# A second copy of k's low part, so that both score products of an attention block take all 128 rows of the array

## The chip, the cores and the metric

The kernel runs on one core of a Trainium2 chip. The time is that of one execution on the device in microseconds (us). The kernel before took 3684.35 us as the median of three runs (3678.03 to 3684.88).

The core has five engines, each with its own queue of instructions that it takes in order: TensorE (PE in the profile) multiplies a moving tile with weights that were loaded into its 128x128 array beforehand (PEld), VectorE (DVE), ScalarE (ACT) and GpSimd (POOL) work elementwise, and SyncE (SP) issues most of the transfers (DMAs). Products land in PSUM, which VectorE and ScalarE read.

## The reference

Two layers of a transformer trunk work on 1024 latent tokens and 256 context tokens of width 1024. In each layer a token mixer (a recurrent part A, a windowed attention B, a neighbourhood attention C) is followed by a mixture of 32 experts. The change touches the scores of the attentions B and C. For the windowed attention the reference computes

```
s_loc = jnp.einsum('bnqhgd,bnkhd->bnhgqk', qb, kb).astype(F32) * ATTN_SCALE
s_ctx = jnp.einsum('bnqhgd,bmhd->bnhgqm', qb, kc).astype(F32) * ATTN_SCALE
p = jax.nn.softmax(jnp.concatenate([s_loc, s_ctx, sink_col], -1), -1).astype(v.dtype)
o = (jnp.einsum('bnhgqk,bnkhd->bnqhgd', p[..., :nk], vb)
     + jnp.einsum('bnhgqm,bmhd->bnqhgd', p[..., nk:nk + L], vc))
```

with heads of 64 numbers. Attention C has the same form with a bias table and no sink.

## The kernel before

q and k are float32 numbers that are stored in two float16 parts: a high part (z = 0) and a low part (z = 1), which is what the high part leaves over. A score q·k is then a sum of products of parts, accumulated in PSUM.

The function `attention` works through six groups in each layer (three of B, three of C), two heads (e = 0, 1) a group. Layer 0 has 10 blocks of 128 queries in a group, layer 1 has 8. For a group these tiles are loaded:

- `qs` (128 partitions): the high part of q in partitions 0 to 63, the low part in 64 to 127.
- `k1` (128 partitions): the high part of k, twice, once in either half (L1100).
- `kl` (64 partitions): the low part of k, once (L1102).
- `vt`: the values.

The groups of B share one load of k, each group of C has its own, so there are four loads of `kl` in a layer.

For each block and head the scores are made in up to three pieces of 256 or 128 keys. A piece is a pair of products into the same PSUM region: L1149 multiplies all 128 rows of `qs` with `k1` (high·high plus low·high), and L1150 multiplies the 64 rows of q's high part with `kl` (high·low). Every product loads its weights, a slice of `qs`, anew. VectorE then adds the mask or bias and finds the maximum (L1162), ScalarE takes the exponential (L1168), GpSimd multiplies with the inverse of the sum (L1179), TensorE transposes the probabilities in pieces of 128 (L1182, L1187), ScalarE and VectorE copy the transposed pieces out of PSUM (L1183, L1188), TensorE multiplies with the values (L1192), whose products use 128 rows and 64 columns of the array, and ScalarE and VectorE write the result in two parts (L1199, L1200). Three blocks can be under way (tiles with three buffers); the scores have two PSUM buffers.

During the groups of B the output of part A (`rwkv_out`, L964 to L1015) runs between the blocks on the same engines. After the last group `out_proj` (L1277) multiplies with the output weights, and the experts follow.

Within a queue the order is fixed when the program is built: a scheduler with a model of the engines lays all instructions of a stage into the queues. A change in a transfer or an operation can therefore move other instructions too.

Of the kernel before, what the change touches and what calls it, by code (L numbers as in the profile page):

```python
# [10 lines left out]
F16 = mybir.dt.float16  # L11
# [10 lines left out]
T = S + L  # L22
P = 128
# [265 lines left out]
class Trunk:  # L289
# [774 lines left out]
    def attention(self, l, ap, qp, sets, with_ctx, groups, depth):  # L1064
        nc = self.nc
        v, g, a, te = nc.vector, nc.gpsimd, nc.scalar, nc.tensor
# [9 lines left out]
        elif groups[0] < 3:  # L1076
            sk, sks, bm = self.attB
            k1, kl, vt = self.attkv
# [5 lines left out]
        for grp in groups:  # L1084
            B = grp < 3
# [5 lines left out]
            qs = qp.tile([P, 2, T], F16, tag="qs", name="qs", bufs=2)  # L1091
# [4 lines left out]
            if not B or i == 0:  # L1096
                kd = self.qkv[c + "k", i].rearrange("(e p) z t -> z p e t", e=2)
                k1 = qp.tile([P, 2, T], F16, tag="k1", name="k1", bufs=1 if B else 2)
                for z in range(2):
                    nc.sync.dma_start(k1[64 * z:64 * z + 64], kd[0])  # L1100
                kl = qp.tile([64, 2, T], F16, tag="kl", name="kl", bufs=1 if B else 2)
                nc.sync.dma_start(kl, kd[1])  # L1102
                vt = qp.tile([P, NT, P], F32, tag="vt", name="vt", bufs=1 if B else 2)
                vd = self.qkv[c + "v", i]
                nb = NT if B else 2
                nc.sync.dma_start(vt[:, 0:nb], vd[0:nb * P].rearrange("(b p) v -> p b v", p=P))

                vg = vd[L:T].rearrange("(r c j) v -> c r j v", c=8, j=8)
                for b in range(nb, NT):
                    nc.sync.dma_start(vt[:, b], vg[b - 2])  # L1110
                self.attkv = k1, kl, vt
# [15 lines left out]
            for blk in range(0 if with_ctx else 2, NT):  # L1127
# [11 lines left out]
                Q = slice(blk * P, blk * P + P)  # L1139
# [6 lines left out]
                for e in range(2):  # L1146
                    pss = ps_s.tile([P, 1024], F32, tag="s", name="pss")
                    for o, k0, n in pieces:
                        te.matmul(pss[:, o:o + n], qs[:, e, Q], k1[:, e, k0:k0 + n], start=True, stop=False)  # L1149
                        te.matmul(pss[:, o:o + n], qs[0:64, e, Q], kl[:, e, k0:k0 + n], start=False, stop=True)  # L1150
                    if not lat:
                        bb = self.zrow.unsqueeze(1).to_broadcast([P, 2, P])
                        o_ap, i_ap = (z.rearrange("p (z k) -> p z k", z=2) for z in (s2[:, e, :nk], pss[:, 0:nk]))
                    else:
                        bb = bias[e][0 if 2 < blk < NT - 1 else 1]
                        o_ap, i_ap = s2[:, e, :nk], pss[:, 0:nk]
                        if blk == 2:
                            bb = bass.AP(tensor=bb.tensor, offset=bb.offset, ap=[bb.ap[0], [384, 2], [1, 256]])
                            o_ap, i_ap = (z.rearrange("p (z k) -> p z k", z=2) for z in (o_ap, i_ap))
                        else:  # L1160
                            bb = bb[:, :nk]
                    v.tensor_tensor_reduce(out=o_ap, in0=i_ap, in1=bb, op0=OP.add, op1=OP.max, scale=1.0,  # L1162
                                           scalar=sks[:, heads[e]:heads[e] + 1] if B else NEG, accum_out=mx[:, e:e + 1])
# [26 lines left out]
                for x, kb in enumerate(kbs):  # L1190
                    for e in range(2):
                        te.matmul(po[64 * e:64 * e + 64, 0:P], vt[:, kb, 64 * e:64 * e + 64], pt[:, e, x * P:x * P + P],  # L1192
                                  start=x == 0, stop=x == len(kbs) - 1)
# [841 lines left out]
```

## Time and profile before

| | |
|---|---|
| median of three runs | 3684.35 us |
| the profiled execution | 3684.05 us, its span 3682.0 us |
| attention, layer 0 | 732.1 to 1035.5 us of the span |
| attention, layer 1 | 2551.0 to 2827.4 us |
| products of L1149 and of L1150 | 552 each |
| granted TensorE clock, mean of the span | 0.91 |

Times in rows are counted from the start of the span. In the rows of an engine's timeline the start of an instruction is measured, while the length given for a matmul is a model that includes the way through the array: successive matmuls overlap. What a matmul takes of TensorE is read from the distance of its start to the next one's. "128*128" and "64*128" are rows and columns of the array that the weights fill. [...]

### The profile page before, as it was taken

To read this page: it belongs to the slowest core of one execution; us is meant where nothing else is said; L and a number is where in the kernel's file an instruction comes from. 1 tells how busy PE (TensorE), PEld (TensorE's weight loads), DVE (VectorE), ACT (ScalarE), POOL (GpSimd) and SP (SyncE) were. 2 spreads that over 40 slices of the span, in tenths; PEclk is the share of its full clock that TensorE was granted. 3 is DMA by queue.
4 is the path that set the end of the run, shared out by engine and by line. 5 is a ranking of instruction groups with operands and counts; after the bars stand their busy time and mean duration, and the time that the engine had idled before them with its cause. 6 is when DMAs were issued, how large, how long until landed. Compare 5 with 4: busy or idle time off the path is not lost. (4 is left out here: it accounts for less than half of the span.)

```text
span 3682.0 us, 67190 instructions
## 1 busy us (share of the span) xinstructions
PE 3146.3 (85%) x26916; PEld 1837.6 (50%) x26916; DVE 1787.3 (49%) x4387; ACT 1090.0 (30%) x2416; POOL 915.9 (25%) x912
## 2 busy tenths in 40 slices
PE   7998889999997889999738988898999879986773
PEld 4656557656654344444326655675655444432331
DVE  4357777377668311111186677773755841110115
ACT  4333334346533100000045433442554310000001
POOL 2023433143324100000073244331432410000003
PEclk9989889989998899999968987997999879997987
DMA  9864333552264889989762533335331778899885
GB/s 361 298 185 113 88 87 95 147 152 67 79 206 166 275 334 360 368 347 358 293 223 74 158 94 98 94 89 163 96 106 57 254 238 344 330 386 360 308 317 196
DMA packets 456087, 770.06 MB, mean 209 GB/s; under 512 B 194398, under 2 KB 328830, under 8 KB 439134
## 3 DMA queue, kind: packets, MB, share of 16 engines
q1 hardware_dynamic: 442206, 718.16, 56.2%
q0 software_dynamic: 12848, 44.97, 3.8%
q8 instruction: 214, 3.51, 0.4%
q10 hardware_dynamic: 720, 2.62, 0.2%
q14 instruction: 99, 0.81, 0.1%
HBM read 650.68 MB, written 114.97 MB: 208 GB/s over the span
## 5 line engine op out<-in xcount | busy, mean ns | idle before, releaser
L1618 PE MATMUL pgate<-wg,hT 128*32 128x256 f32 (+2 forms) x1968 | 532.4, 487 | 85.9 <-issue 31.8
L1618 PEld LDWEIGHTS pgate<-wg,hT 128*32 128x32 f32 (+2 forms) x1968 | 196.3, 135 | 349.9 <-issue 287.7
L1618 PE MATMUL pgate<-wu,hT 128*32 128x256 f32 (+1 forms) x1648 | 361.6, 462 | 10.2 <-DMA wu<-w_up 10.2
L1639 PE MATMUL pd<-wd,gT 128*32 128x256 f32 (+2 forms) x1968 | 321.8, 472 | 51.7 <-DVE gT L1631 25.8
L514 PE MATMUL acc<-hL,wH 128*128 128x256 f16 (+2 forms) x1040 | 345.5, 333 | 16.3 <-POOL hL L471 16.2
L513 PE MATMUL acc<-hH,wH 128*128 128x256 f16 (+2 forms) x1040 | 343.3, 334 | 7.2 <-DVE hH L470 6.4
L515 PE MATMUL acc<-hH,wL 128*128 128x256 f16 (+2 forms) x1040 | 344.9, 333 | 0.0
L1623 ACT ACTIVATE sg<-pgate 64x256 f32<-64x256 f32 (+2 forms) x86 | 43.1, 501 | 980.3 <-PE pgate L1618 980.3
L1592 POOL DMA_INDIRECT xg<-hmoe,map x69 | 62.3, 903 | 1037.5 <-PE ptg L1628 566.3
L1179 POOL TENSOR_SCALAR s<-s,rd 128x640 f32<-128x640 f32 (+2 forms) x216 | 171.6, 795 | 288.4 <-DVE rd L1175 115.8
L1639 PEld LDWEIGHTS pd<-wd,gT 128*32 128x32 f32 (+2 forms) x1968 | 127.1, 130 | 208.7 <-issue 123.0
L1624 DVE TENSOR_TENSOR sg<-sg,pgate 64x256 f32<-64x256 f32 (+1 forms) x66 | 35.6, 540 | 344.4 <-ACT sg L1623 340.9
L1168 ACT ACTIVATE s<-s,nm 128x640 f32<-128x640 f32 (+2 forms) x216 | 164.4, 764 | 45.8 <-DVE nm L1165 39.8
L1277 PE MATMUL acco<-wo,o 128*128 128x512 f16 x756 | 176.5, 387 | 0.0
L1192 PE MATMUL po<-pt,vt 128*64 128x128 f32 x1920 | 168.6, 291 | 7.3 <-DVE pt L1183 6.5
L1618 PE MATMUL pup<-wu,hT 128*128 128x512 f32 x320 | 165.4, 605 | 9.6 <-DMA wu<-w_up 9.6
L1149 PE MATMUL pss<-k,qs 128*128 128x256 f16 (+1 forms) x552 | 153.2, 278 | 17.3 <-DMA k<-Bk 13.4
L1624 DVE TENSOR_TENSOR sg<-sg,pup 128x512 f32<-128x512 f32 x20 | 13.8, 688 | 292.1 <-PE pup L1618 292.1
L1618 PEld LDWEIGHTS pgate<-wu,hT 128*32 128x32 f32 (+1 forms) x1648 | 134.3, 123 | 42.1 <-issue 21.1
L1150 PE MATMUL pss<-kl,qs 64*128 64x256 f16 (+1 forms) x552 | 152.6, 277 | 0.0
L515 PEld LDWEIGHTS <-wL 128*128 128x128 f16 (+1 forms) x1040 | 104.9, 101 | 87.4 <-issue 26.7
L513 PEld LDWEIGHTS <-wH 128*128 128x128 f16 (+1 forms) x1040 | 105.4, 101 | 75.4 <-issue 19.7
(406 smaller groups left out, 6435.3 us busy)
## 6 DMA issues: line engine op xcount, KB each, us to landing
wu<-w_up SPq DMA_DIRECT2D x64, 2048.0 KB
wd<-w_down SPq DMA_DIRECT2D x64, 2048.0 KB
wg<-w_gate SPq DMA_DIRECT2D x64, 2048.0 KB
wmod<-w_mod SPq DMA_DIRECT2D x96, 512.0 KB
w<-w_in SPq DMA_DIRECT2D x41, 512.0 KB
ld<-ys SPq DMA_DIRECT2D x40, 384.0 KB
z<-inv SPq DMA_DIRECT2D x80, 128.0 KB
ys<-y SPq DMA_DIRECT2D x20, 512.0 KB
```

The source lines that it names most:

```text
L513: self.nc.tensor.matmul(ov, H[:, k, :], hh, start=k == 0, stop=False)
L514: self.nc.tensor.matmul(ov, H[:, k, :], hl, start=False, stop=False)
L515: self.nc.tensor.matmul(ov, Lo[:, k, :], hh, start=False, stop=k == KD - 1)
L1149: te.matmul(pss[:, o:o + n], qs[:, e, Q], k1[:, e, k0:k0 + n], start=True, stop=False)
L1150: te.matmul(pss[:, o:o + n], qs[0:64, e, Q], kl[:, e, k0:k0 + n], start=False, stop=True)
L1168: a.activation(s2[:, e, :nk], s2[:, e, :nk], AF.Exp, bias=nm[:, e:e + 1], scale=1.0 / SS, accum_out=den[:, e:e + 1])
L1179: g.tensor_scalar(s2[:, e, :nk], s2[:, e, :nk], rd[:, e:e + 1], SC_Q, OP.mult, OP.mult)
L1192: te.matmul(po[64 * e:64 * e + 64, 0:P], vt[:, kb, 64 * e:64 * e + 64], pt[:, e, x * P:x * P + P], start=x == 0, stop=x == len(kbs) - 1)
L1277: te.matmul(acc, o[:, zo, k] if k < KD - 1 else self.og_last[:, zo, tok], wo[:, zw, k, c], start=k == 0 and y == 0, stop=k == KD - 1 and y ...
L1592: nc.gpsimd.indirect_dma_start(out=xg[:m], out_offset=None, in_=self.h2[l], in_offset=bass.IndirectOffsetOnAxis(ap=idx, axis=0))
L1618: te.matmul(o[off + i * m:off + i * m + m, :n], hT[:, k], w[:, k, i * n:i * n + n], start=k == 0, stop=k == KD - 1)
L1639: te.matmul(o, gT[:, k, :m], wd[:, k, i * n:i * n + n], start=k == 0, stop=k == 3)
```

## The change

`kl` becomes a tile of 128 partitions, which two transfers fill with the same low part of k, and L1150 (L1151 now) multiplies all 128 rows of `qs` with it. It thereby also adds the product low·low. The weights of both products of a piece are now the same slice of `qs`. All line numbers from L1103 on are higher by one.

```
-                kl = qp.tile([64, 2, T], F16, tag="kl", name="kl", bufs=1 if B else 2)
-                nc.sync.dma_start(kl, kd[1])
+                kl = qp.tile([P, 2, T], F16, tag="kl", name="kl", bufs=1 if B else 2)
+                for z in range(2):
+                    nc.sync.dma_start(kl[64 * z:64 * z + 64], kd[1])
...
                         te.matmul(pss[:, o:o + n], qs[:, e, Q], k1[:, e, k0:k0 + n], start=True, stop=False)
-                        te.matmul(pss[:, o:o + n], qs[0:64, e, Q], kl[:, e, k0:k0 + n], start=False, stop=True)
+                        te.matmul(pss[:, o:o + n], qs[:, e, Q], kl[:, e, k0:k0 + n], start=False, stop=True)
```

On SyncE, ahead of the first group of layer 0, the queue before has these rows (`k_9029` is the tile `k1`, `Bk_0` the array with k, `Ck_0` an array with k of attention C that is still being written):

```order
L1095 DMA qs<-Bq_0_3628 64x1280 x4
L1100 DMA k_9029<-Bk_0_5158 64x2x1280 x2
L1102 DMA kl<-Bk_0_5158 64x2x1280
L1060 DMA Ck_0_8222<-qhl 256x1x512
L1106 DMA vt<-Bv_0_2957 128x10x128
L1095 DMA qs<-Bq_0_4138 64x1280 x4
```

and now these:

```order
L1095 DMA qs<-Bq_0_3628 64x1280 x4
L1100 DMA k_9029<-Bk_0_5158 64x2x1280 x2
L1103 DMA kl<-Bk_0_5158 64x2x1280
L1060 DMA Ck_0_8222<-qhl 256x1x512
L1103 DMA kl<-Bk_0_5158 64x2x1280
L1107 DMA vt<-Bv_0_2957 128x10x128
L1095 DMA qs<-Bq_0_4138 64x1280 x4
```

The second half of `kl` stands behind the store of `Ck_0`, and the values behind it.

On TensorE the pairs of the scores stay in their order, but the scheduler places the steps of `rwkv_out` and of the softmax differently between them. In the first group of layer 0 the second tile of `rwkv_out` (L992) stands here before:

```order
L1149 MATMUL pss<-k_9029,qs 128x128
L1150 LDWEIGHTS qs
L1150 MATMUL pss<-kl,qs 128x128
L1192 MATMUL po<-pt,vt 64x128 x3
L1182 MATMUL pp<-c_58,s_9115 128x128 x8
L992 MATMUL po<-c_58,yb 64x64 x16
L1149 LDWEIGHTS qs
L1149 MATMUL pss<-k_9029,qs 128x256
```

and here now:

```order
L1150 MATMUL pss<-k_9029,qs 128x128
L1151 LDWEIGHTS qs
L1151 MATMUL pss<-kl,qs 128x128
L1188 MATMUL pp_9272<-c_58,s_9228 128x128 x2
L1193 MATMUL po<-pt,vt 64x128 x8
L1183 MATMUL pp<-c_58,s_9289 128x128 x4
L992 MATMUL po<-c_58,yb 64x64 x16
L1193 MATMUL po<-pt,vt 64x128 x2
```

Ahead of that tile stand 20 pairs of scores before and 38 now, so it has moved back by three blocks.

## Rows read from the trace of the kernel before

**Rows 1.** The page: busy time of TensorE, its share of the span, instructions.

```profile
PE 3146.3 (85%) x26916; PEld 1837.6 (50%) x26916; DVE 1787.3 (49%) x4387; ACT 1090.0 (30%) x2416; POOL 915.9 (25%) x912
```

**Rows 2.** Busy time by stretch: first group, rest of B, C, for each layer.

```profile
core 0: us, PE busy (x) PEld busy (x) DVE busy (x) ACT busy (x) POOL busy (x), PEclk, DMA share, GB/s
732.10:789.40 57.30, 53.37 (x328) 29.67 (x325) 41.83 (x140) 25.73 (x72) 23.33 (x26) 0.79 0.73 190
789.40:889.20 99.80, 98.45 (x817) 60.30 (x815) 72.33 (x242) 55.35 (x162) 41.80 (x50) 1.00 0.21 64
889.20:1035.50 146.30, 141.79 (x1129) 89.49 (x1127) 91.72 (x270) 85.49 (x219) 53.53 (x72) 0.98 0.27 76
2551.00:2599.20 48.20, 48.20 (x274) 26.27 (x274) 28.49 (x91) 19.35 (x51) 14.41 (x16) 0.65 0.81 225
2599.20:2691.30 92.10, 91.66 (x769) 57.07 (x767) 64.55 (x215) 50.40 (x140) 38.75 (x44) 1.00 0.26 81
2691.30:2827.40 136.10, 130.65 (x1026) 82.80 (x1024) 79.71 (x216) 74.40 (x182) 44.26 (x60) 0.95 0.30 90
```

**Rows 3.** TensorE's longest waits, layer 0 then layer 1: total us, times, longest.

```profile
PE pss L1149 <- DVE mx L1162: 3.9, 4, 1.6
...
PE pss L1149 <- DMA k<-Bk: 13.4, 1, 13.4
PE po L1192 <- DVE pt L1183: 5.3, 8, 3.4
```

**Rows 4.** VectorE's waits in the attention of layer 0, same columns.

```profile
DVE pt L1183 <- PE pp L1182: 34.3, 32, 2.3
...
DVE s L1162 <- PE pss L1150: 14.3, 29, 1.4
```

**Rows 5.** TensorE's timeline, layer 0, group of C: start us, length us, instruction.

```profile
945.83 0.27 PE L1182 MATMUL pp<-c,s 128*128 128x128 f32 x1
945.94 0.27 PE L1149 MATMUL pss<-k,qs 128*128 128x256 f16 x1
946.14 0.28 PE L1150 MATMUL pss<-kl,qs 64*128 64x256 f16 x1
946.36 0.28 PE L1149 MATMUL pss<-k,qs 128*128 128x256 f16 x1
```

**Rows 6.** TensorE's timeline, layer 0, a piece of 128 keys.

```profile
858.35 0.23 PE L1149 MATMUL pss<-k,qs 128*128 128x128 f16 x1
858.51 0.23 PE L1150 MATMUL pss<-kl,qs 64*128 64x128 f16 x1
```

**Rows 7.** TensorE's timeline, layer 0, input projection, 256 columns.

```profile
699.54 0.27 PE L513 MATMUL acc<-hH,wH 128*128 128x256 f16 x1
699.65 0.27 PE L514 MATMUL acc<-hL,wH 128*128 128x256 f16 x1
```

**Rows 8.** TensorE's timeline, layer 0, input projection, 128 columns.

```profile
712.52 0.22 PE L524 MATMUL accn<-wH,hH 128*128 128x128 f16 x1
712.58 0.22 PE L525 MATMUL accn<-wH,hL 128*128 128x128 f16 x1
```

**Rows 9.** Lines L1149 and L1150: count, shortest/median/longest ns, first and last start.

```profile
L1149 PEld LDWEIGHTS <-qs x552: 95/96/152, 732.1 to 2815.7; 128*128 128x128 f16 x184
L1149 PE MATMUL pss<-k,qs x552: 219/282/421, 732.1 to 2815.7; 128*128 128x256 f16 x160, 128*128 128x128 f16 x24
...
L1150 PE MATMUL pss<-kl,qs x552: 226/280/417, 732.4 to 2815.9; 64*128 64x256 f16 x160, 64*128 64x128 f16 x24
```

**Rows 10.** Loads of kl: their issues on SyncE, and the size of one.

```profile
L1102 SPq DMA_DIRECT2D kl<-Bk x2: 573/574/574, 711.7 to 2546.4; - x2
...
kl<-Bk SPq DMA_DIRECT2D x1, 320.0 KB
```

**Rows 11.** TensorE's timeline, layer 1, first group, clock at half.

```profile
2557.78 0.40 PE L1149 MATMUL pss<-k,qs 128*128 128x256 f16 x1
2558.11 0.39 PE L1150 MATMUL pss<-kl,qs 64*128 64x256 f16 x1
```

## The prediction

> **What bounds the kernel now.** I began with the page's busy times: TensorE is busy for 85% of the span and none of the others for more than half of it [rows 1]. An average over stages does not say what an edit in attention is worth, so I read the busy times by stretch. In the six stretches of attention TensorE is busy in 564 of 580 us (their sum), VectorE in 65% on the whole, 73% in the first stretch [rows 2]. Next the waits. TensorE waits 13.4 us for k ahead of layer 1's first score, but within the attentions its longest entries are 3.9 and 5.3 us in total [rows 3]. VectorE stands for TensorE again and again: 34.3 us for transposes and 14.3 us for scores in layer 0 alone [rows 4]. TensorE therefore sets the pace here, and time taken from it can be gained.
>
> Busy matmuls overlap, so I then read distances between starts. After a transpose, which fills 128x128, the first score product starts 0.11 us later. From that product to its partner with 64 rows it is 0.20 us, and from there to the next one with 128 rows 0.22 us [rows 5]. In the input projection, where every product has 128 rows and its own weights too, products of the same 256 columns follow each other at 0.11 us [rows 7]. With 128 columns the same holds: 0.16 us from 128 to 64 rows [rows 6] against 0.06 us where the rows stay 128 [rows 8]. So each passage between 128 and 64 rows costs 0.16 - 0.055 = 0.215 - 0.11 = 0.105 us, whatever the number of columns, and in both directions. (0.215 and 0.055 are the means over a run of such starts; the rows round to hundredths.)
>
> **The change part by part.**
>
> *The passages.* There are 552 pairs [rows 9]. The old order of instructions has a passage inside each: 552. A second product is followed directly by the next pair's first one 392 times, and by a transpose with 128x128 65 times; those passages go too. Where a product with the values follows (128 rows, 64 columns; some 85 times) the array changes its shape as before, and I count nothing. That makes 1009 passages x 0.105 = 106 us of TensorE's time. With the clock at half the pair's distance is 0.33 us [rows 11] where 256 columns without a passage would take twice 0.11 = 0.22; the passage costs 0.11 us there as well, so one price will do.
>
> [...] The row first: the weight load of a score product takes 96 ns [rows 9], nearly the price of the passage, so the 0.105 us could be a load that is not hidden. [...] The trace disagrees: the projection's products share all rows and still follow at 0.11 us [rows 7]. [...]
>
> *How much of it reaches the end.* In proportion to the pairs (48 in a group of layer 0, 44 in layer 1) the six stretches of [rows 2] could lose 9.2, 18.4, 27.6, 8.4, 16.9 and 25.3 us. That leaves 48.1, 81.4, 118.7, 39.8, 75.2 and 110.8 us, in which VectorE's unchanged work fills 87, 89, 77, 72, 86 and 72%. [...] The products with the values wait for copies that stood behind 1.2 us of scores and now behind 0.55 us. Where VectorE comes to 85% or more I let 60% of the gain through, elsewhere 85%. Both shares are chosen; they lie between 100% and 40%. At 40% VectorE would be busy for (91.7 + 79.7) / (282.4 - 21.2) = 66% of the stretches of C, hardly more than the 61% of now, so less than that would need a cause that the rows don't show. The sum: 5.5 + 11.0 + 23.5 + 7.1 + 10.1 + 21.5 = 78.7 us. With 40% everywhere it would be 42, with all of it 106.
>
> *The loads.* Eight more transfers of 320 KB [rows 10]. At the rate of the two first groups, 190 and 225 GB/s [rows 2], one takes 1.7 and 1.5 us. In these groups the DMA engines are loaded to 73 and 81%, layer 1 waits for k as it is [rows 3], and the scores need both halves of `kl`; I put both on the path: 3.2 us. From below it is nothing, if other instructions fill the time. If the store of `Ck_0` ahead of the second half holds it up as well, I allow a second transfer's time, so 6.4 us is the upper bound. The six loads of C run ahead under groups whose transfers are busy for 21 to 30%; without that cover they would cost 6 x 1.6 = 10 us. The issue of a load, 0.6 us on SyncE [rows 10], lies ahead of the need except in the first groups, and is in the 3.2 us.
>
> *The order.* The steps of `rwkv_out` move back by some blocks in the groups of B. Their work is the same, and they still end within the B groups; I cost it at nothing. Its cover is TensorE's backlog; without this, VectorE's steps of one such tile would come in one piece ahead of a block's maximum. VectorE waits up to 2.3 us at a time now [rows 4], and with nine tiles 20 us is the worst, which is part of the rival on VectorE.
>
> *Sum.* 3684.05 - 78.7 + 3.2 = 3608.6 us on the profiled execution. That execution lies 0.3 us below the median of the runs, so I predict 3609 us. After the attention each layer goes on with the output weights and experts, whose loads wait for space that attention frees, so a saved microsecond passes on to the end.
>
> **The rivals.**
>
> *VectorE and the chain of softmax take over.* Only 40% of the gain gets through: 3684 - 42 + 3 = 3645 us. For it: VectorE at 86 to 89% in half of the stretches, and few buffers (two for scores, three blocks). Against it: 49 us of VectorE's idle time in layer 0 are waits for TensorE itself [rows 4], which shrink with it. Chance 0.19.
>
> *Everything gets through, and the clock gains.* In layer 1's first group the clock is granted at 0.65, after the wait of 13.4 us [rows 3], and it stays low while TensorE is shown as busy throughout [rows 2]; denser products may lift it earlier. If that group ran at full clock for half of its slow time it would be some 8 us: 3684 - 106 + 3 - 8 = 3573 us. Against it: the waits of [rows 3] grow when TensorE reaches them sooner. Chance 0.11.
>
> *The price is the weight load, not the change of rows.* Then the distances remain 0.2 us and only the transfers are added: 3684 + 3 = 3687 us. Against it: a score product behind a transpose, also with its own load, starts after 0.11 us [rows 5], and the projection keeps that pace [rows 7]. Chance 0.03.
>
> *The clock falls (slower).* TensorE with less to do waits more, and the clock of attention, 0.93 as the mean of [rows 2] weighted by length, falls. Its work at full clock would be about 580 - 106 = 474 us, and each share of it that moves to half clock costs as much again. If all six stretches had the 0.79 of the first, 2 x (0.93 - 0.79) = 0.28 more of it would be slow: 474 x 0.28 = 133 us, and the time 3684 - 103 + 133 = 3714 us. It decides from a mean clock of 0.93 - 103/474/2 = 0.82 on. For it: the lowest clock, 0.65, follows the longest wait. Against it: 1.00 in two stretches in spite of waits of up to 1.6 us [rows 2, 3]. Chance 0.04.
>
> **How the numbers follow.** The forecast has 0.63, with a range of its own of 3592 to 3629 us (from 90 to 55% of the 106 us in all stretches alike, with the 3.2 us for the loads). The range to hold 8 in 10 reaches to the rival on VectorE and to the one in which all gets through: 3572 to 3650 us. What a measurement can tell from no change is about 0.2%, 7 us here. The forecast and the first two rivals are faster by more: 0.93. No change 0.03, slower 0.04.
>
> **What would show it.** [...] The stretches of [rows 2] should take 53.5, 89, 123, 42.6, 82 and 115 us, and their difference must be that of the whole. TensorE's waits for L1162's maximum and for L1183's copies should grow from a few us to some 25, the part of the gain that does not get through; 60 would be the rival on VectorE. The first score with `kl` should come 1.5 us after the old one. The prediction is wrong if the distances stay, if the granted clock of attention falls below 0.85, or if the gain of attention is lost in the experts after it.

## The result, and the profile after

The changed kernel takes 3595.57 us (median of four runs, 3594.50 to 3606.41), the kernel before 3682.19 us (four runs): the ratio is 0.9773, its 95% interval 0.9756 to 0.9790, a gain of 77 to 90 us. The forecast was 3609 us, in a range of 3572 to 3650.

The steps first. This is TensorE's timeline of the changed kernel in a group of C, the counterpart of [rows 5] and [rows 6]:

```profile
937.82 0.27 PE L1193 MATMUL po<-pt,vt 128*64 128x128 f32 x1
938.02 0.66 PE L1183 MATMUL pp<-c,s 128*128 128x128 f32 x4
...
938.95 0.27 PE L1150 MATMUL pss<-k,qs 128*128 128x256 f16 x1
939.06 0.27 PE L1151 MATMUL pss<-kl,qs 128*128 128x256 f16 x1
939.17 0.22 PE L1150 MATMUL pss<-k,qs 128*128 128x128 f16 x1
939.23 0.22 PE L1151 MATMUL pss<-kl,qs 128*128 128x128 f16 x1
939.28 0.27 PE L1150 MATMUL pss<-k,qs 128*128 128x256 f16 x1
```

Score products now follow each other at 0.11 us with 256 columns and at 0.055 us with 128, within pairs and between them, where it was 0.20 to 0.22 and 0.16. Products with the values, which fill 128x64, still stand 0.20 us ahead of a transpose with 128x128.

The busy times by stretch answer to [rows 2], with the same columns. The granted clock (PEclk) is a share of full speed; in the traces of both kernels it is 0.50 or 1.00 at any one time, so a mean between the two is a stretch that had both:

```profile
730.10:784.60 54.50, 44.37 (x327) 30.25 (x325) 40.83 (x128) 26.08 (x73) 24.80 (x26) 0.78 0.82 222
784.60:873.30 88.70, 81.76 (x816) 61.55 (x814) 72.48 (x254) 54.40 (x161) 40.96 (x48) 0.96 0.24 74
873.30:998.90 125.60, 117.56 (x1130) 90.35 (x1128) 89.68 (x270) 84.41 (x219) 53.44 (x72) 0.97 0.32 91
2507.10:2545.50 38.40, 31.46 (x310) 24.52 (x311) 27.72 (x96) 20.02 (x54) 15.36 (x16) 0.90 0.95 268
2545.50:2628.70 83.20, 74.95 (x725) 56.88 (x724) 65.17 (x205) 47.62 (x133) 38.20 (x42) 0.96 0.38 102
2628.70:2743.60 114.90, 103.32 (x1034) 82.14 (x1031) 78.61 (x222) 74.27 (x183) 45.67 (x60) 0.96 0.39 113
```

Their lengths add up to 505.3 us, before 579.8: the attentions are 74.5 us shorter. The work of the other engines is the same (VectorE 374 us, before 379); TensorE's busy time falls from 564 to 453, and it no longer fills its stretches. Where it waits shows in its waits, layer 0 and then layer 1, against [rows 3]:

```profile
PE po L1193 <- DVE pt L1184: 8.0, 9, 3.8
PE pss L1150 <- DVE mx L1163: 6.8, 7, 3.0
...
PE pss L1150 <- DMA k<-Bk: 15.0, 1, 15.0
PE pss L1150 <- DVE mx L1163: 12.6, 6, 5.2
PE po L1193 <- DVE pt L1184: 7.2, 8, 1.9
...
PE pss L1151 <- DMA kl<-Bk: 0.3, 1, 0.3
```

The two waits for VectorE's maximum and for its copies are 34.6 us together. Before they were 10.3: the maximum had 3.9 us in layer 0, the copies 1.1 there and 5.3 in layer 1.

The profiled executions differ by 87.3 us in span, 12.8 more than the attentions. No edit was made to that remainder. It was 3102 us before and 3089 after, and over the fourteen profiles of this study (twelve more below) it lay between 3078 and 3108 us. The 12.8 us are within that scatter, but they came again: the changed kernel profiled a second time (e13 below) has 3085 us, and in both profiles some 7 us are missing between the two attentions and 3.5 behind the second one. The interval of the timed gain also starts at 77 us, above the 74.5 of the attentions. I have not traced where these microseconds come from.

### The profile page after: what moved, and what is told of

Its sections match the earlier page's. It is cut to its first block, busy times and chain, and to the rows that moved or that the text cites. A ratio compares the mean times of both kernels' runs of the same rounds, so it can differ in the third digit from the quotient of the medians.

```text
span 3594.7 us, 67193 instructions
## 1 busy us (share of the span) xinstructions
PE 3032.4 (84%) x26916; PEld 1834.2 (51%) x26916; DVE 1782.3 (50%) x4387; ACT 1086.5 (30%) x2416; POOL 922.2 (26%) x912
## 4 chain that ended last, share of the span: by engine, by line
PE 41%; DVE 19%; DMA 15%; issue 4%; SPq 2%; ACT 2%; POOL 1%; DVEq 0%; ACTq 0%; POOLq 0%
PE pgate L1619 10%; DMA ys<-y 7%; PE pd L1640 6%; PE pup L1619 4%; PE po L1193 3%; DMA wu<-w_up 3%; PE pp L1183 2%; PE acc L513 1%; PE acc L515 1%; PE acc L514 1%; SPq L1581 1%; PE pss L1150 1%; PE pss L1151 1%; DVE s L1163 1%; DVE il L940 1%
## 5 line engine op out<-in xcount | busy, mean ns | idle before, releaser
L1180 POOL TENSOR_SCALAR s<-s,rd 128x640 f32<-128x640 f32 (+2 forms) x216 | 172.8, 800 | 208.2 <-DVE rd L1176 77.0
L1150 PE MATMUL pss<-k,qs 128*128 128x256 f16 (+1 forms) x552 | 127.7, 270 | 34.6 <-DVE mx L1163 19.4
L1193 PEld LDWEIGHTS po<-pt,vt 128*64 128x64 f32 x1920 | 117.7, 141 | 55.8 <-DVE pt L1184 21.6
L1644 DVE TENSOR_TENSOR y<-pd,ge 128x512 f32<-128x512 f32 (+1 forms) x43 | 24.1, 561 | 241.5 <-DMA ys<-y 178.5
```

What stands on the lines that cost most here:

```text
L1180: g.tensor_scalar(s2[:, e, :nk], s2[:, e, :nk], rd[:, e:e + 1], SC_Q, OP.mult, OP.mult)
```

## The experiments

"Attention" is read from each profile: from the first score product of a layer to the first product of `out_proj`. "Clock" is the granted clock of the first 30 us of layer 1's attention, as a share of full speed. The ratio is to the kernel before on the same chip, with its 95% interval.

| kernel | ratio (interval) | attention, layer 0 + 1, us | clock |
|---|---|---|---|
| before | 1 | 303.6 + 276.6 = 580.2 | 0.50 |
| changed | 0.9773 (0.9756 to 0.9790) | 269.0 + 236.7 = 505.7 | 0.87 |
| e1 loads only | 1.0003 (0.9980 to 1.0025) | 306.2 + 282.5 = 588.7 | 0.50 |
| e2 pairs alternate | 0.9888 (0.9852 to 0.9924) | 284.0 + 254.8 = 538.8 | 0.51 |
| e3 both products on 64 rows | 0.9860 (0.9825 to 0.9896) | 281.5 + 246.8 = 528.3 | 0.61 |
| e4 one product | 0.9715 (0.9678 to 0.9752) | 251.8 + 222.5 = 474.3 | 0.89 |
| e6 copies on ScalarE | 0.9803 (0.9786 to 0.9821) | 276.1 + 249.3 = 525.4 | 0.84 |
| e7 the same, on before | 1.0094 (1.0076 to 1.0112) | 316.8 + 298.6 = 615.4 | 0.50 |
| e8 values on 128 columns | 0.9909 (0.9888 to 0.9931) | 291.7 + 258.1 = 549.8 | 0.94 |
| e9 e6 and e8 | 0.9894 (0.9873 to 0.9914) | 295.9 + 266.1 = 562.0 | 0.85 |
| e10 four score blocks | 0.9744 (0.9707 to 0.9781) | 258.2 + 227.2 = 485.4 | 0.86 |
| e11 three score buffers in PSUM | 0.9845 (0.9803 to 0.9886) | 283.8 + 251.9 = 535.7 | 0.87 |
| e12 first group first | 0.9783 (0.9747 to 0.9819) | 263.0 + 246.1 = 509.1 | 0.65 |
| e13 changed again | 0.9758 (0.9716 to 0.9799) | 269.5 + 236.7 = 506.2 | 0.93 |

**e1: the loads without the rows.**

```
-                        te.matmul(pss[:, o:o + n], qs[:, e, Q], kl[:, e, k0:k0 + n], start=False, stop=True)
+                        te.matmul(pss[:, o:o + n], qs[0:64, e, Q], kl[0:64, e, k0:k0 + n], start=False, stop=True)
```

> The changed kernel with its tile of 128 partitions and both loads of kl, but the second product on 64 rows again (qs and kl rows 0 to 63). It tells the loads and the shifted order apart from the rows of the product. Theory 1 (the gain is the passages between 128 and 64 rows that went): the passages are back, score products 0.215 us apart, the two attentions together 576 to 588 us as before (580), the whole 3678 to 3692 us; the loads by themselves cost 3 us at most. Rival (the gain comes from the new order of the queues, not from the rows): much of the gain stays, under 3640 us. A weight load that is not hidden would give the same as theory 1 here.

The time is that of the kernel before, within 0.25%. The timeline has the old distances, 0.20 and 0.22 us:

```profile
950.06 0.27 PE L1150 MATMUL pss<-k,qs 128*128 128x256 f16 x1
950.26 0.28 PE L1151 MATMUL pss<-kl,qs 64*128 64x256 f16 x1
950.48 0.28 PE L1150 MATMUL pss<-k,qs 128*128 128x256 f16 x1
```

So the loads did not make the gain: with the 64 rows put back, and the loads kept, the attention is 83 us longer than in the changed kernel. The order is answered only in part. e1's queues were laid out anew, and in layer 0 the second tile of `rwkv_out` stands behind 26 pairs of scores, between the 20 of before and the 38 of the changed kernel. e2 below shows whether a gain needs the new order. The profiled attention was 8.5 us longer than before, just beyond the 588 us that I had expected at most; with the timed runs equal I don't make a price of that.

**e2: the same products, every second pair turned round.**

```
+                    for j, (o, k0, n) in enumerate(pieces):
+                        two = [(slice(0, P), k1), (slice(0, 64), kl)]
+                        if (j + e * len(pieces)) % 2:
+                            two.reverse()
+                        for y, (r, kk) in enumerate(two):
+                            te.matmul(pss[:, o:o + n], qs[r, e, Q], kk[:, e, k0:k0 + n], start=y == 0, stop=y == 1)
```

> The kernel before, where every second pair of score products does the 64-row product first (128, 64 | 64, 128 | 128, 64). Same products, same loads, same sums in another order. By the order of instructions 587 passages between 128 and 64 rows remain of about 1010, so 420 go, both kinds alike. Theory 1 (a passage costs 0.105 us, about 70% of TensorE's gain reaches the end, as in the change: 74.5 of 106): 44 us of TensorE, 31 us of the whole, 3651 us (3640 to 3662). Pairs of equal rows 0.11 us apart, unequal ones 0.215. Rival (0.1 us is each product's weight load on the same q, not hidden): nothing, 3682 us (3676 to 3688). If only the way from 128 to 64 rows costs: 552 such passages become 271 and it comes to 21 us; if only the way back: 392 become 273 and some 15 us, with the distances showing which.

3639.3 us, ratio 0.9888. These rows are the clearest of the study, since e2 is the kernel before in all but the order of two lines; the tiles of `rwkv_out`, too, stand behind as many pairs of scores as before (20, 50, 74 and 98 in layer 0):

```profile
959.56 0.27 PE L1153 MATMUL pss<-k,qs 128*128 128x256 f16 x1
959.77 0.39 PE L1153 MATMUL pss<-kl,qs 64*128 64x256 f16 x2
960.09 0.34 PE L1153 MATMUL pss<-k,qs 128*128 128x256 f16 x2
960.36 0.23 PE L1153 MATMUL pss<-kl,qs 64*128 64x128 f16 x1
```

From 128 to 64 rows it is still 0.21 us. The two products of 64 rows are shown as one entry; this is the second:

```profile
959.89 0.27 PE L1153 MATMUL pss<-kl,qs 64*128 64x256 f16 x1
```

They are 0.12 us apart, and the way back to 128 rows takes the 0.20 us up to 960.09. Both directions cost, some 0.08 us each against the products of equal rows beside them. Of the 44 us that 420 passages are worth, the attention kept 580.2 - 538.8 = 41.4 in the profile; the interval of the timed runs allows 28 to 55.

**e3: both products on 64 rows.** It leaves out the product of q's low part with k's high part.

```
-                        te.matmul(pss[:, o:o + n], qs[:, e, Q], k1[:, e, k0:k0 + n], start=True, stop=False)
+                        te.matmul(pss[:, o:o + n], qs[0:64, e, Q], k1[0:64, e, k0:k0 + n], start=True, stop=False)
```

> The kernel before with the first score product on 64 rows too (it leaves out the part low q times high k). Every pair is then 64 rows, 64 rows; passages remain at the ways in and out. Theory 1 (it is the change of rows, not 64 rows as such): inside and between pairs 943 passages go, 119 at the way in from transposes are new, net 824 x 0.105 = 86 us of TensorE, of which 70% come through: 3622 us (3608 to 3640), distances 0.11 us within and between pairs. Rival (a product on 64 rows is slow whatever stands before it): distances 0.2 us or more, 3680 us or slower. Rival (weight load not hidden): distances stay 0.2 us, 3682 us.

```profile
950.07 0.38 PE L1187 MATMUL pp<-c,s 128*128 128x128 f32 x2
950.38 0.28 PE L1149 MATMUL pss<-k,qs 64*128 64x256 f16 x1
950.50 0.27 PE L1150 MATMUL pss<-kl,qs 64*128 64x256 f16 x1
950.61 0.27 PE L1149 MATMUL pss<-k,qs 64*128 64x256 f16 x1
```

Products of 64 rows follow each other at 0.11 us like those of 128. The dear place is now the way in: the second transpose starts at 950.18 (0.11 us after the first), the first score 0.20 us later. Theory 1 holds; 64 rows are not slow as such, and no weight load shows. The time, 3628.9 us, is 7 above the estimate. The attention lost 51.9 us of the 86 of TensorE, and its granted clock was 0.90 in both layers against 0.95 and 0.91 before.

**e4: the changed kernel with one product in place of two.** It leaves out the parts with k's low part.

```
-                        te.matmul(pss[:, o:o + n], qs[:, e, Q], k1[:, e, k0:k0 + n], start=True, stop=False)
-                        te.matmul(pss[:, o:o + n], qs[:, e, Q], kl[:, e, k0:k0 + n], start=False, stop=True)
+                        te.matmul(pss[:, o:o + n], qs[:, e, Q], k1[:, e, k0:k0 + n], start=True, stop=True)
```

> The changed kernel without the second score product (it leaves out the parts with k's low part); its loads stay. It takes another 408 x 0.107 + 144 x 0.055 = 51.6 us from TensorE and nothing from the other engines, and so asks what holds the attention after the change. Theory A (TensorE still sets the pace, as before the change): 65 to 80% of it come through, 3554 to 3562 us. Theory B (VectorE and the chain of softmax have taken over): less than 30%, 3580 us or more, and TensorE's waits for L1163's maximum and L1184's copies at least double from 38 us. My own mean between them: VectorE in the groups of B, TensorE in those of C, some 25 us, 3570 us.

3575.7 us, 20 us less than the changed kernel by the medians, 39% of the 51.6; in the profile the attentions lost 505.7 - 474.3 = 31.4 us, 61%. By either that is between the theories. TensorE still holds part of the time after the change, and its waits did not double: there is more to gain from it, at a worse rate than in e2.

**e6 and e7: the copies of VectorE on ScalarE, on the changed kernel and on the one before.**

```
-                    (a.copy if e == 0 else v.tensor_copy)(pt[:, e, 0:nf * P], pp[:, 0:nf * P])
+                    a.copy(pt[:, e, 0:nf * P], pp[:, 0:nf * P])
```

> The changed kernel with both copies of the transposed probabilities (L1184) on ScalarE; before, VectorE had the second head's. It takes 12 x 6.3 = 75 us of work from VectorE (374 us in 505 us of attention) and gives ScalarE 70 us more (307 to 377), nothing changes on TensorE. Theory B (VectorE's queue holds the attention after the change): the attentions get 15 to 30 us shorter, the whole 3566 to 3581 us, and TensorE's waits for VectorE's maximum and copies shrink. Theory A (TensorE holds it): within 5 us of 3595. Rival C (the chain of softmax holds it, whichever engine does a step): no gain, or slower by up to 15 us, because ScalarE's exponentials queue behind the copies.

> The same edit on the kernel before. There TensorE set the pace by my reading, and VectorE's work was under cover: within 5 us of 3680 us whichever theory holds for the changed kernel. A gain of over 10 us here would say that VectorE already held part of the attention before the change.

In the profile both became slower than what they were made from: e6 has 525.4 us of attention in place of 505.7, e7 615.4 in place of 580.2. The timed runs show it for e7 (1.0094); e6's interval still touches that of the changed kernel. VectorE did lose work, as its column (third) shows for e6's two attentions, 324 us against 374, and ScalarE's (fourth) rose from 307 to 354. TensorE (first), on which I had expected no change, is busy for 467 us in place of 453, and its waits for VectorE's maximum came to 33.5 us in place of 19.4:

```profile
727.00:1003.10 276.10, 245.97 (x2269) 179.86 (x2267) 175.72 (x591) 189.74 (x512) 116.34 (x146) 0.96 0.39 110
2501.90:2751.20 249.30, 220.69 (x2065) 165.96 (x2066) 148.51 (x472) 164.72 (x418) 100.09 (x118) 0.94 0.45 127
```

So the gain that theory B forecast did not come. That does not clear the amount of VectorE's work, because the edit also loaded ScalarE: the same edit cost 35 us of attention on the kernel before (e7) and 20 us here, and the 15 us between could be what less work for VectorE is worth after the change. No run tells the two apart. Nor was e7 neutral, as I had expected: moving this step of the softmax from one queue to another costs, even where TensorE sets the pace. That it costs because the copies stand among the exponentials is my reading.

**e8 and e9: the values on 128 columns** (e9 with e6's edit as well).

```
+                vt = qp.tile([P, NT, 2, P], F32, tag="vt", name="vt", bufs=1)
+                for e in range(2):
+                    g.memset(vt[:, :, e, 64 - 64 * e:128 - 64 * e], 0.0)
...
-                        te.matmul(po[64 * e:64 * e + 64, 0:P], vt[:, kb, 64 * e:64 * e + 64], pt[:, e, x * P:x * P + P],
-                                  start=x == 0, stop=x == len(kbs) - 1)
+                        te.matmul(po[:, 0:P], vt[:, kb, e], pt[:, e, x * P:x * P + P],
+                                  start=x == 0 and e == 0, stop=x == len(kbs) - 1 and e == 1)
```

> The changed kernel, whose products with the values take all 128 columns too: the values of a head stand beside 64 columns of zeros, both heads add into the same region of PSUM, so the result is the same. The values have one buffer in C (two before) and are loaded in halves. 375 passages between 128 and 64 columns go (by the order of instructions), 0.095 us each, 35 us of TensorE; the products go from 0.20 to 0.22 us for two heads, 9 us back. Theory 1 widened to columns: net 26 us of TensorE, of which 40 to 60% come through as in the last part of the change, 3580 to 3586 us; starts from products with the values to transposes at 0.11 in place of 0.203 us. Rival (a passage of columns costs nothing and the 0.2 us are the way through the array): distances stay, the time rises by 9 us and by late values, 3600 us or more.

> The last two edits together on the changed kernel: less work for VectorE and fewer passages on TensorE. If VectorE's queue is what held back the gain (theory B), the two add up or do better, since what TensorE saves now comes through: 3548 to 3565 us. If the chain of softmax holds it (rival C), no more than the better one alone, 3580 us or over.

A miss, by 75 us (3658.7; by the ratio some 66, as the kernel before, too, took 8 us longer beside it), and the fault is in my price. The late values are not the reason: TensorE waits for them for 0.6 us in all. The passages of columns do go:

```profile
949.43 0.83 PE L1199 MATMUL po<-pt,vt 128*128 128x128 f32 x6
950.10 1.04 PE L1189 MATMUL pp<-c,s 128*128 128x128 f32 x8
```

Six starts 0.11 us apart put the last one at 949.99, and the transpose follows 0.11 us after it, where the changed kernel has 0.20. But two heads' products in the two halves of the columns had run side by side: in the changed kernel the second head's product mostly starts 0.006 us after the first's, and the next pair 0.10 us later. On 128 columns they run one after the other. The busy time of the products with the values, in both attentions, shows it; first the changed kernel (TensorE first):

```profile
730.10:998.90 268.80, 91.22 (x1008) 62.32 (x1008) 0.93 0.40 112
2507.10:2743.60 236.50, 77.60 (x912) 55.32 (x912) 0.95 0.48 134
```

then e8:

```profile
731.20:1022.90 291.70, 137.72 (x1008) 124.69 (x1008) 0.96 0.37 106
2540.80:2798.80 258.00, 123.90 (x912) 112.10 (x912) 0.97 0.42 115
```

168.8 us became 261.6. I had counted 9 us back for them; it was 93, against 35 saved. e9, with e6's edit as well, is no better, 3652.6 us.

**e10 and e11: more blocks under way, or more PSUM for the scores.** e10 gives the scores four buffers and the transposed probabilities two (three and three before):

```
-                s2 = ap.tile([P, 2, 640], F32, tag="s2", name="s2", bufs=depth)
+                s2 = ap.tile([P, 2, 640], F32, tag="s2", name="s2", bufs=4)
...
-                pt = ap.tile([P, 2, 640], F32, tag="pt", name="pt", bufs=depth)
+                pt = ap.tile([P, 2, 640], F32, tag="pt", name="pt", bufs=2)
```

> The changed kernel with four buffers for the scores and their small tiles (three before) and two for the transposed probabilities (three before), so a fourth block may be under way up to the transposes. Theory D (what holds the gain back after the change is the number of blocks under way): 10 to 20 us faster than the changed kernel on the same chip, and its waits for the maximum shrink. Theory E (the order of work within a block and two PSUM buffers for the scores): within 6 us of the changed kernel, or slower where two buffers for the probabilities are too few.

e11 replaces, for the groups of C, the pools of PSUM:

```
+        e_pss.close()
+        e_pss, pss = opened("psS2", bufs=3, space=PSUM)
+        e_pst, pst = opened("psT2", bufs=2, space=PSUM, side="right")
```

> The changed kernel with three PSUM buffers for the scores and two for transposes and products with the values in the groups of C (two and four before). Theory E' (TensorE's wait for L1163's maximum, 19 us in total, is for a free score buffer): in C it falls, 5 to 10 us faster than the changed kernel. Rival (the other side's buffers are as scarce): the waits move to transposes and products, same or slower; the groups of B, unedited, stay.

e11 is slower, 3625.6 us, with 15.4 us of waits for L1184's copies in layer 0 where the changed kernel has 8.0: the other side's buffers were as scarce. Its waits for the maximum, which were to fall, are 20.1 us where the changed kernel has 19.4. e10 has the shortest attention of all kernels that compute the same:

```profile
734.00:992.10 258.10, 234.67 (x2268) 178.11 (x2266) 206.04 (x651) 164.36 (x452) 118.97 (x146) 0.97 0.42 116
2504.30:2731.50 227.20, 205.66 (x2064) 160.94 (x2064) 173.45 (x520) 142.23 (x370) 98.48 (x118) 0.97 0.49 140
```

485.4 us, 20.8 less than e13 beside it, and TensorE's waits for the maximum, in its two layers, are down to 9.5 us, from 18.2 in e13:

```profile
PE pss L1150 <- DVE mx L1163: 6.0, 7, 2.7
...
PE pss L1150 <- DVE mx L1163: 3.5, 4, 2.1
```

The waits for the maximum are as theory D has them. But they are not what the 20.8 us are made of. e13's attentions, with the same columns:

```profile
725.70:995.20 269.50, 244.79 (x2268) 182.63 (x2266) 203.00 (x651) 165.04 (x452) 118.99 (x146) 0.93 0.39 112
2503.40:2740.10 236.70, 207.89 (x2065) 161.77 (x2066) 172.47 (x520) 141.79 (x370) 98.92 (x118) 0.96 0.47 134
```

TensorE stands idle for 53.5 us there and for 45.0 in e10, so 8.5 us came out of all waits together. The other 12.3 us are its busy time, 452.7 against 440.3 for the same products, with the clock of layer 0 at 0.97 in place of 0.93. Why the clock was higher, these runs do not show, and e10's queues also have another order. The timed runs do not settle it either: 3591.9 us against 3596.6, within the 6 us of theory E, and the intervals of the two ratios overlap almost wholly. e10's profile has 3103 us outside attention, e13's 3085, both inside the range named above, so the 20 us drown in it. e10 may be the best kernel here; shown is only that its attention was shorter in one profile.

**e12: the first group written ahead of `rwkv_out`.**

```
+        self.attention(l, ap, qp, [(pss, pst)], not last, range(1), 3)
         self.rwkv_out(l, range(1 if last else 0, T // 256), rp, psr, "r")
-        self.attention(l, ap, qp, [(pss, pst)], not last, range(3), 3)
+        self.attention(l, ap, qp, [(pss, pst)], not last, range(1, 3), 3)
```

> The changed kernel, where the first group's attention is written ahead of rwkv_out, so that the loads of q, k and kl come first in the queue. In layer 1 TensorE waits 15 us for k. If the loads ahead of it in the queue are what delays k: the wait falls by 4 to 8 us, and the whole by 4 to 8 (3588 to 3592 on a chip where the changed kernel takes 3596). If the transfers wait for space that the input projection frees: no gain, and rwkv_out, now later, may cost up to 5 us.

In layer 1 the wait for k fell by 10 us, while 2.7 us went to `kl`:

```profile
PE pss L1150 <- DMA k<-Bk: 5.2, 1, 5.2
...
PE pss L1151 <- DMA kl<-Bk: 2.7, 1, 2.7
```

But k did not come sooner. From the end of layer 0's attention to layer 1's first score it is 1507.5 us here, 1508.0 in the changed kernel and 1508.1 in e13; counted from the same point, TensorE finished the input projection some 9 us later, and so waited less. Layer 1's attention grew by 9 us: 3605.9 us, not faster. Its first 30 us had a lower clock (0.65, e13 0.93) and less work in them (TensorE was busy for 19.5 us, in e13 for 24.1); the run does not tell what each cost.

**e13: the changed kernel beside the last three.**

> The changed kernel once more, beside the last three on the same chip, to measure them against. 0.975 to 0.980 of the kernel before; attention 500 to 512 us, and in layer 1 a full clock within 6 us of the first score, where kernels with passages between 128 and 64 rows took 29 to 44 us.

Ratio 0.9758, attention 506.2 us: the result came again in another set of runs. In layer 1 the clock is granted at 0.50 for the first 4.4 us and at 1.00 up to the 30th, as expected.

## Why the prediction was right, and where it was not

**The passages.** Right in price and cause. Starts at 0.11 and 0.055 us, as the old trace showed for products that share their rows; TensorE's busy time in the six stretches falls by 564 - 453 = 111 us; some 8 of them go with the clock of one stretch (below), and the rest is close to the 106 of the forecast. e2 takes passages away by order alone and gains 41 of 44 us, e3 takes them away with 64 rows throughout. The rival by which the weight loads would show is out: in the changed kernel every pair has the same rows, and a load of its own (98 ns as the median, before 96 and 93), and still starts 0.11 us apart. In e2, e3 and e8 each change of rows or columns adds 0.08 to 0.10 us; what the array does in that time, no row shows.

**How much gets through.** The forecast was 75.5 us for the attentions with the loads, the trace says 74.5. The six stretches were to take 53.5, 89, 123, 42.6, 82 and 115 us and took 54.5, 88.7, 125.6, 38.4, 83.2 and 114.9. That the sums agree so well is in part luck: five stretches together lost 4.4 us less than forecast, and layer 1's first group 4.2 us more, with the clock that I had held apart as a rival.

The reason that I gave for the missing third is not borne out. I let less through where VectorE is fuller; e6 took 50 us of work from VectorE and gained nothing, though it loaded ScalarE in return. In the six stretches TensorE saved 111 us and its idle time grew from 15.7 to 51.9, so 36 us did not come. Its waits for maxima and copies account for 24 of them, from some 10 us to 35 (I had said 25); the rest is spread over other waits, such as those for GpSimd's L1180 (7.7 us, before 1.4). Of what TensorE's busy time saved, 91% reached the attention's time in e2, 76% in e3 and 67% in the change, and of e4's further 44 us 71%. So the first part came through almost whole and the rest at a lower rate. That three blocks under way cover the first part and no more is my reading, not shown: in e10 a fourth block took 8.5 us out of the waits, and that edit also changed the buffers of the probabilities and the order.

**The clock.** I held a gain from the clock apart as a rival. It came in one place: layer 1's first group lost 9.8 us where 5.6 were forecast, with its clock at 0.90 in place of 0.65 [rows 2]. TensorE's busy time there fell by 16.7 us, of which the passages are worth 8.4 by the forecast's price; the other 8.3 fit the 8 us that I had named in the rival. Elsewhere the clock hardly moved: 0.96 to 0.97 in three stretches that had 0.98 to 1.00, 0.78 and 0.96 in two that had 0.79 and 0.95. The mean by length is 0.94, before 0.93, so the rival of a falling clock did not come. Its 474 us of work "at full clock" were in fact worked out at 0.93, which made it look a little dearer than it is.

**The loads.** 3.2 us were forecast. Layer 1's wait for k grew from 13.4 to 15.0 us, and the products' wait for `kl` came to 0.3. The first score with `kl` in layer 1 started 2.8 us after the first score, before 2.4, and not 1.5 us later: a tile of `rwkv_out` stands between the two in both kernels and covers most of the load. e1's profile has 8.5 us more attention than before and its timed ratio, 1.0003, leaves room for nothing up to some 9 us, so the 3.2 are neither confirmed nor refuted.

**The order.** Costed at nothing. e2 gains its 41 us with the tiles of `rwkv_out` where they stood before, so the gain does not need the new order. What the changed kernel's own order is worth by itself, no run tells; e1's order is another. The 20 us that I called the worst came from VectorE's longest wait in layer 0, 2.3 us; in layer 1 it waited up to 4.9 us at a time, so that bound was too low.

**The rest of the 86.6 us** was not forecast. The sign that the stretches' difference must be that of the whole was not met: the remainder of the program is 12.8 us shorter, 17 in e13, within a range of 30 over all kernels. This is nearly all of the 13 us by which the forecast of 3609 lies above the measured 3595.6. Whether it belongs to the change stays open.

## What to carry to other kernels

Read distances between starts, not lengths of matmuls: here "busy" hid 106 us of gaps on an engine that looked full. Where a product uses fewer rows or columns than its neighbours (here 0.20 to 0.22 us between starts in place of 0.11), either fill it up, if the extra terms are harmless, or sort the products by shape; but first look whether the narrow ones ran side by side, as the two heads' products with the values did (169 us of busy time, against 262 in e8). And when the bounding engine gets faster, don't expect the whole of the saving: here the first 46 us of it came through at 91%, all 111 us at 67%.

## What the runs showed of the hardware that was not expected

**In layer 1 the clock came back later in kernels with passages.** Both kernels enter layer 1's attention at a granted clock of 0.50 after TensorE's wait for k, 13.4 us before and 15.0 in the changed kernel, and so does e13 after 15.3 us for `kl`. All four with passages between the two products of a pair (before, e1, e2, e7) had 0.50 or 0.51 over the next 30 us, though TensorE is shown as busy throughout, for 29.99 to 30.00 us; e3, with 64 rows in both products, had 0.61; the eight with 128 rows (e4 with one product) and the groups in the old order had 0.84 to 0.94. Before, in three parts:

```profile
2551.00:2570.00 19.00, 19.00 (x80) 8.60 (x81) 7.18 (x20) 5.66 (x14) 5.06 (x5) 0.50 1.09 325
2570.00:2584.60 14.60, 14.60 (x72) 8.59 (x71) 8.54 (x29) 5.30 (x14) 4.47 (x5) 0.50 0.81 213
2584.60:2599.00 14.40, 14.40 (x124) 9.01 (x124) 12.57 (x44) 8.19 (x22) 4.68 (x6) 1.00 0.44 110
```

and the changed kernel from its first score:

```profile
2507.00:2526.00 19.00, 15.86 (x142) 11.94 (x144) 13.47 (x40) 9.71 (x25) 7.24 (x8) 0.88 1.09 326
```

The engine that is shown as busy for all of 19 us did 80 matmuls at a granted clock of 0.50; with the passages gone it did 142, with gaps, at a granted clock of 0.88. Passages alone do not decide it: e12 has none between 128 and 64 rows and had 0.65, and in the first group of layer 0 the kernel before and the changed one had 0.79 and 0.78. What does decide, the runs do not tell.

**Two products in the two halves of the columns run side by side** (e8: 169 us of busy time against 262 for the same sums one after the other), so a narrow shape can be worth its passages.
